# Decoder block on one core: single-use banks for the u and down sums, partition moves by GpSimd DMAs, and a scheduler charge for changes of TensorE's shape

## The chip, the cores and the metric

One core of a Trainium2 chip. The metric is device microseconds of one execution; three runs of the kernel before gave 388.19 to 389.34 us, median 389.16. The profile is of one further execution.

## The reference, cut

One layer on x of 256 tokens by 1024 channels, in float32. A projection gives Q, K, V (512 columns each), u (512) and two gates (1024 each). Q and K get a rotary turn of 16 of each head's 64 dimensions; attention is causal over one block of 256, 8 heads. u goes through a diagonal state-space model (S5, 32 groups of 16 channels, 64 states), a gelu and a gated unit:

```python
proj = h @ w_in[l]
q, k, v, u, g_attn, g_ssm = jnp.split(proj, splits, axis=-1)
attn = moba_attention(q, k, v)
...
y = (jnp.einsum('ghp,bsgp->bsgh', c_re, h_re) - jnp.einsum('ghp,bsgp->bsgh', c_im, h_im) + d_skip * uf)
y = jax.nn.gelu(y.reshape(bsz, seq, SSM_WIDTH))
y = y * jax.nn.sigmoid(y @ w_glu)
...
merged = sigmoid(g_attn) * (attn @ w_attn_proj[l]) + sigmoid(g_ssm) * (ssm @ w_ssm_proj[l])
mix = merged @ w_out[l]
h = layer_norm(DEEPNORM_ALPHA * h + mix, ln1_g[l], ln1_b[l])
up = causal_depthwise_conv(h @ w_up[l], conv_w[l], conv_b[l])
val, gate = jnp.split(up, 2, axis=-1)
ff = (jax.nn.gelu(gate) * val) @ w_down[l]
h = layer_norm(DEEPNORM_ALPHA * h + ff, ln2_g[l], ln2_b[l])
```

## The kernel before, in words

**Products.** Most products are made in three parts: ACT copies a float32 tile to float32r (`hi`), DVE subtracts it from the tile (`lo`), and TensorE (PE) sums hi x hi, lo x hi and hi x lo (`split_to`, L486; `three`). Weights arrive by 512 KB loads from SP into a ring of three raw buffers and are split into a ring of hi/lo pairs (`chunk`). The u projection alone is made in plain float32 (`u_sum`): 8 k tiles by 4 sums of 128 x 256, each product passing the array four times.

**Banks.** PSUM is held as six one-bank tiles and one tile of two banks, `twin`. `J` is the first two banks (bank_61 and bank_62 in orders), `AT` the next three (63 to 65), `S5` the two halves of `twin` and bank_66. The four u sums lie in `J` and the two halves of `twin` (L573).

**u and y change partitions.** The state-space part wants groups of 32 channels at other partitions than the projection leaves them. After u is summed, 32 ACT copies of 32 x 128 bring it from PSUM to `uc` (L711 to L717), splitting even from odd tokens on the way. `e_operand` and `toeplitz` make the SSM's operands out of transposes and small float32 products; `ssm_unit` (L882, four of them) multiplies `uc` side by side on halves of the array into `twin`, and DVE scans. `ssm_out` (L912, two halves) sums y and evicts each half with 16 ACT gelus of 32 x 128, to other partitions and interleaved tokens again. `y` is then split to hi and lo for the gated unit.

**The tail.** The down projection's sums are `dacc` (L1141): two of 512 columns for the first 128 tokens, in AT[0] and AT[1]; 512, 256 and 256 columns for the rest, in AT[2] and the two halves of `twin`. The products of the last few tiles are made part by part, and each part is evicted by DVE (`gm`, scalar_tensor_tensor) into the last layer norm.

**What sets the order.** All operations are recorded first (`Recorder`, L104). A dependence is found by the region of memory (`_region`, L87), in PSUM by the bank of 512 floats; an engine that reads a bank and another that writes it follow each other. `forward` (L156) then plays the engines through with a cost for each operation, and of several such orders the one that ends first is issued, engine by engine. So a changed cost, bank or operation moves instructions all over the program. DVE and GpSimd (Pool) are taken to exclude each other (`SHARED`, L151). In the trace nearly every DVE instruction is of L300, ACT's of L376, matmuls of L395 (sums), L414 (single), L423 (side by side), transposes of L430, SP's loads of L441.

Of the kernel before, what the change touches and what calls it, by code (L numbers as in the profile page):

```python
# [20 lines left out]
P = 128  # L21
# [65 lines left out]
def _region(ap):  # L87
    row = ap.ap[0][0]
    lo = ap.offset % row
    if _in_psum(ap):  # L90

        end = lo + sum((n - 1) * s for s, n in ap.ap[1:])
        return (ap.tensor.name, 0, P, lo // 512 * 512, end // 512 * 512 + 512)
    return (ap.tensor.name, ap.offset // row, ap.offset // row + ap.ap[0][1],
            lo, lo + sum((n - 1) * s for s, n in ap.ap[1:]) + 1)


class Op:
    __slots__ = ("i", "eng", "fn", "cost", "dur", "func", "dma", "group", "preds", "succs", "start", "end")


class Recorder:
# [4 lines left out]
    def add(self, eng, fn, outs, ins, cost, dur=None, func=None, group=None):  # L107

        o = Op()
        o.i, o.eng, o.fn, o.cost, o.func = len(self.ops), eng, fn, cost, func  # L110
        o.dur, o.dma, o.group = dur, dur is not None, group
        o.preds, o.succs = set(), []
        for write, aps in ((False, ins), (True, outs)) if group is None else ((True, outs), (False, ins)):
            for ap in aps:
                t, p0, p1, a, b = _region(ap)
                psum = _in_psum(ap)
                log = self.mem.setdefault(t, [])
                keep = []
                for e in log:
                    q0, q1, c, d, j, w = e  # L120
                    if q0 < p1 and p0 < q1 and c < b and a < d:
                        if w and write and group is not None and self.ops[j].group is group:
                            keep.append(e)
                            continue
                        if (w or write or (psum and self.ops[j].eng != eng)) and j != o.i:
                            o.preds.add(j)
                        if write and p0 <= q0 and q1 <= p1 and a <= c and d <= b:
                            continue
                    keep.append(e)
                keep.append((p0, p1, a, b, o.i, write))  # L130
                self.mem[t] = keep
            if group is not None and write:

                if group.before is None:
                    group.before = set(o.preds)
                o.preds |= group.before
        o.preds.discard(o.i)
        self.ops.append(o)
        return o
# [16 lines left out]
    def forward(self, key, wait=0.0, margin=0.0):  # L156


        ops = self.ops
        left = [len(o.preds) for o in ops]  # L160
        ready_at = [0.0] * len(ops)
        engs = sorted({o.eng for o in ops})
        free = dict.fromkeys(engs, 0.6)
        cand = {e: [] for e in engs}
        table, dma = None, 0.0

        cold, win, busy = True, 0, 0.0
        for o in ops:
            if not left[o.i]:
                cand[o.eng].append(o.i)  # L170
        done = 0
        while done < len(ops):
            best = None
            for e in engs:
                if cand[e]:
                    t = max(free[e], min(ready_at[i] for i in cand[e]))
                    if best is None or t < best[0]:
                        best = (t, e)
            t, e = best
            c = cand[e]  # L180
            if e == "SP":
                i = min(c)
            else:
                i = min((i for i in c if ready_at[i] <= t + 0.02), key=lambda i: (key[i], i))
                if wait:
                    until = t + wait * ops[i].cost
                    j = min((i for i in c if ready_at[i] <= until), key=lambda i: (key[i], i))
                    if key[j] < key[i] - margin:
                        i = j
            c.remove(i)  # L190
            o = ops[i]
            cost = o.cost
            if o.func in self.SETS and table not in self.SETS[o.func]:
                table = self.SETS[o.func][0]
                cost += 1.3
            t = max(t, ready_at[i])
            if e == "PE":
                n = int(t / self.WINDOW)
                if n != win:
                    use = busy / self.WINDOW  # L200
                    cold = n > win + 1 or use < 0.42 or (cold and use < 0.75)
                    win, busy = n, 0.0
                if cold:
                    cost *= 2
                busy += min(t + cost, (win + 1) * self.WINDOW) - t
            o.start = t
            free[e] = t + cost
            if e in self.SHARED:

                e2 = self.SHARED[e]  # L210
                free[e2] = max(free[e2], t + cost)
            if o.dma:
                dma = max(dma, t + cost + 0.65) + o.dur
                o.end = dma + 0.93
            else:
                o.end = t + cost
            done += 1
            for j in o.succs:
                ready_at[j] = max(ready_at[j], o.end + self.latency(o, ops[j]))
                left[j] -= 1  # L220
                if not left[j]:
                    cand[ops[j].eng].append(j)
        return max(o.end for o in ops)
# [158 lines left out]
class Pe:  # L382
# [34 lines left out]
    def side_by_side(self, rounds):  # L417


        def issue():  # L420
            for products in rounds:
                for o, l, r, start, stop in products:
                    self.real.matmul(o, l, r, start=start, stop=stop)  # L423

        flat = [q for products in rounds for q in products]
        self.rec.add("PE", issue, [q[0] for q in flat], [x for q in flat for x in q[1:3]],
                     0.1 + sum(0.12 + 1.17e-3 * max(_free(q[0][0]), 128) for q in rounds))

    def transpose(self, o, a, eye):
        self.rec.add("PE", lambda: self.real.transpose(o, a, eye), [o], [a, eye], 0.109)  # L430


class Dma:
# [13 lines left out]
def block_kernel(ctx: ExitStack, tc: tile.TileContext, w, xtok, small, lnv, out):  # L447
# [1 line left out]
    rec = Recorder()  # L449
    V, G = Vec(rec, nc.vector), Gps(rec, nc.gpsimd)  # L450
    A, T = Act(rec, nc.scalar), Pe(rec, nc.tensor)
    SP = Dma(rec, nc.sync)

    pool = ctx.enter_context(tc.tile_pool(name="pool", bufs=1))
    ps = ctx.enter_context(tc.tile_pool(name="ps", bufs=1, space=PSUM))
# [19 lines left out]
            self.items = [i for i in self.items if not any(i is j for j in items)]  # L475

    J, AT, S5 = banks[0:2], banks[2:5], [twin[:, 0], twin[:, 1], banks[5]]
    pj, at, s5 = Ring(J), Ring(AT[2:] + AT[:2]), Ring(S5)
    pjw = Ring([J[0], S5[2], J[1], AT[0], AT[1]])
    pju = Ring([J[0], J[1], S5[2]])  # L480

# [88 lines left out]
    hilo.more(late[0], late[1])  # L570


    u_acc = J + S5[0:2]  # L573
    xr = gt

    def x_piece(k0, k1):
# [131 lines left out]
    tt(tau_l, tau, tau_h, SU)  # L708


    for q in range(4):  # L711
        for i4 in range(4):
            i = 4 * q + i4
            for j in range(2):
                b0 = 64 * (i % 2) + 32 * j
                src = u_acc[q][32 * i4:32 * i4 + 32, j:S:2]
                A.copy(uc[b0:b0 + 32, i // 2], src)  # L717

# [156 lines left out]
            A.copy(tz[r0, ms, 32:64], pv[r0, :, par, 1])  # L877
            tt(tz[r1, ms, 32:64], pv[r1, :, par, 0], di[r1, ms], AD)

    y = again(et[0], (4, S))  # L880

    def ssm_unit(un):  # L882

# [28 lines left out]
    def ssm_out(big):  # L912
# [4 lines left out]
        def term(n, k, par):  # L917
# [3 lines left out]
            if n == 2:  # L921
# [4 lines left out]

        T.side_by_side([[term(n, k, par) for par in range(2)] for k in range(4) for n in range(2)]
                       + [[term(2, k, par) for par in range(2)] for k in range(4)])
        for k in range(4):
            for par in range(2):  # L930
                i = 8 * big + 2 * k + par
                for j in range(2):
                    b0 = 64 * par + 32 * j
                    c0 = 32 * (i % 4)
                    A.activation(y[c0:c0 + 32, i // 4, j:S:2],
                                 py[par][b0:b0 + 32, k * P:(k + 1) * P], AF.Gelu_apprx_tanh)


    mask = col("mask").unsqueeze(1).to_broadcast([P, 2, P])
# [83 lines left out]
    yh, yl = yhl[:, 0], yhl[:, 1]  # L1023
    sh, sl = shl[:, 0], shl[:, 1]
    for k in range(4):
        split_to(yh[:, k], yl[:, k], y[:, k])
    for cc in range(2):
        hi, lo = chunk(C_GLU + cc)
        for mi in range(2):
            m = 2 * cc + mi  # L1030
            acc = pj()
            def wk(k):
                c = slice(k * 256 + mi * P, k * 256 + (mi + 1) * P)
                return hi[:, c], lo[:, c]
            T.product(acc[:, :S], three(wk, lambda k: (yh[:, k], yl[:, k]), range(4)))
            th_ = tmp["cvv"]()
            A.activation(th_, acc[:, :S], AF.Tanh, scale=0.5)
            stt(th_, th_, 1.0, y[:, m], op0=AD, op1=MU)
            split_to(sh[:, m], sl[:, m], th_)


# [96 lines left out]

    conv = col("conv").rearrange("p (m k) -> p m k", k=4)
    DCOLS = [[(0, 512), (512, 1024)], [(0, 512), (512, 768), (768, 1024)]]  # L1140
    dacc = [[AT[0], AT[1]], [AT[2], S5[0][:, 0:256], S5[1][:, 0:256]]]  # L1141
    d_sum = [[T.sum(b) for b in q] for q in dacc]


# [39 lines left out]
        if LAG <= i < NF - LAST + LAG:  # L1184
            down(i - LAG, all_parts)

    for part in all_parts:
        for i in range(NF - LAST, NF):
            down(i, [part])


    halves = [slice(nh * 512, (nh + 1) * 512) for nh in range(2)]
# [118 lines left out]
```

## Time and profile before

| what | value |
|---|---|
| median of three runs | 389.16 us (388.19 to 389.34) |
| the profiled execution, its own time | 389.81 us |
| its span | 387.4 us |
| PE, DVE, ACT busy, share of the span | 95%, 81%, 62% |
| granted TensorE clock, mean | 0.992 |

A row of a timeline or group gives the engine, the line, the operation with output and inputs by the program's names, the shape, and in brackets the engine's idle time just before it with what ended it. A matmul row's busy time runs from the first start to the last (modelled) end, and records overlap, so paces are taken from start to start. A record with 256 columns of plain float32 stands for half a product.

### The profile page before, as it was taken

Reading aid. Unit: us, or ns where it says so; the run is one execution under the profiler, and the core shown is the slowest. Engines: PE = TensorE matmul, PEld = TensorE weight load, DVE = VectorE, ACT = ScalarE, POOL = GpSimd, SP = SyncE. Lnnn points to the kernel's source line nnn. Section 1 sums busy time; section 2 is a strip of 40 time slices with the busy share of each in tenths; the row PEclk is TensorE's granted clock in tenths of the full one; section 3 lists DMA queues with packets and bytes.
Section 4 is the critical chain, followed back from the end, with each engine's and each line's share of the span. In section 5 each row is a group of like instructions: output and inputs, shape, how many; then the busy total and the mean of one; then the engine's idle time right before and its main releaser. Section 6 shows DMA issues by size and latency. Waiting matters only on the chain.

```text
span 387.4 us, 7089 instructions
## 1 busy us (share of the span) xinstructions
PE 369.7 (95%) x2734; PEld 338.3 (87%) x2734; DVE 314.2 (81%) x580; ACT 240.1 (62%) x447; POOL 7.1 (2%) x48
## 2 busy tenths in 40 slices
PE   7899999999999999999899999999999999999990
PEld 6677777889889999979899999999999999999970
DVE  4979768999699967978999997777776777777775
ACT  3489988957997567622637656555555556555620
POOL 6000000000000000000000000000000000000000
PEclk9999999999999999999999999999999999999996
DMA  7913565413533653698157775545465645554002
GB/s 264 360 61 113 194 216 183 164 57 144 184 111 115 227 203 108 196 338 283 36 170 229 248 239 187 199 164 207 175 197 187 212 168 186 195 180 146 2 0 108
DMA packets 19184, 67.35 MB, mean 174 GB/s; under 512 B 2256, under 2 KB 2512, under 8 KB 19152
## 3 DMA queue, kind: packets, MB, share of 16 engines
q1 hardware_dynamic: 19152, 66.91, 50.1%
q8 instruction: 21, 0.34, 0.3%
q14 instruction: 11, 0.09, 0.1%
HBM read 65.86 MB, written 1.05 MB: 173 GB/s over the span
## 4 chain that ended last, share of the span: by engine, by line
PE 62%; DVE 15%; ACT 13%; DMA 7%; issue 2%; SPq 1%; DVEq 0%; ACTq 0%
PE bank L395 54%; DMA raw<-w 7%; PE twin L395 5%; DVE wl L300 3%; ACT wh L376 3%; ACT et L376 2%; PE bank L423 1%; DVE gm L300 1%; ACT uc L376 1%; SPq L441 1%; ACT L376 1%; ACT p L376 1%; DVE sa L300 1%; ACT gm L376 1%; DVE qk L300 1%
## 5 line engine op out<-in xcount | busy, mean ns | idle before, releaser
L300 DVE TENSOR_TENSOR wl<-raw,wh 128x1024 fp32r<-128x1024 f32 x65 | 79.2, 1223 | 11.3 <-ACT wh L376 11.2
L376 ACT ACTIVATE wh<-raw 128x1024 fp32r<-128x1024 f32 x65 | 68.0, 1053 | 16.7 <-PE bank L395 7.9
L300 DVE SCALAR_TENSOR_TENSOR qk<-bank,sml,qk 128x255 f32<-128x255 f32 (+1 forms) x88 | 42.0, 482 | 26.8 <-ACT qk L376 25.3
L376 ACT ACTIVATE qk<-bank,sml 128x256 f32<-128x256 f32 x44 | 24.8, 565 | 57.7 <-PE bank L395 57.7
L395 PE MATMUL bank<-shl,wh 128*128 128x256 f32 x336 | 48.1, 281 | 0.0
L395 PEld LDWEIGHTS bank<-shl,wh 128*128 128x128 f32 x336 | 42.9, 188 | 0.5
L395 PE MATMUL bank<-yhl,wh 128*128 128x256 f32 x304 | 42.9, 280 | 0.0
L395 PE MATMUL bank<-yhl,wl 128*128 128x256 f32 x288 | 39.8, 279 | 0.0
L395 PEld LDWEIGHTS bank<-yhl,wh 128*128 128x128 f32 x304 | 38.8, 188 | 0.1
L395 PEld LDWEIGHTS bank<-yhl,wl 128*128 128x128 f32 x288 | 36.3, 189 | 0.0
L395 PE MATMUL bank<-wh,xh 128*128 128x512 f32 (+1 forms) x102 | 31.3, 376 | 0.6 <-ACT wh L376 0.5
L395 PE MATMUL bank<-wh,xl 128*128 128x512 f32 (+1 forms) x102 | 29.7, 367 | 0.0
L395 PE MATMUL bank<-wl,xh 128*128 128x512 f32 (+1 forms) x102 | 29.2, 371 | 0.0
L300 DVE TENSOR_TENSOR wl<-ctab,wh 128x1024 fp32r<-128x1024 f32 x18 | 22.0, 1222 | 1.9 <-ACT wh L376 1.8
L395 PEld LDWEIGHTS bank<-wh,xh 128*128 128x128 f32 x102 | 17.7, 188 | 4.4 <-ACT wh L376 1.5
L395 PEld LDWEIGHTS bank<-wh,xl 128*128 128x128 f32 x102 | 18.1, 188 | 2.9
L376 ACT ACTIVATE xh<-stab 128x1024 fp32r<-128x1024 f32 x14 | 14.7, 1051 | 9.1 <-PE twin L395 9.1
L395 PEld LDWEIGHTS bank<-wl,xh 128*128 128x128 f32 x102 | 17.3, 188 | 3.2 <-DVE wl L300 0.4
L376 ACT ACTIVATE wh<-ctab 128x1024 fp32r<-128x1024 f32 x18 | 18.9, 1052 | 1.7 <-PE twin L395 1.5
L300 DVE TENSOR_TENSOR xl<-stab,xh 128x1024 fp32r<-128x1024 f32 x14 | 17.1, 1223 | 1.9 <-ACT xh L376 1.9
L395 PE MATMUL bank<-yhl,xh 128*128 128x256 f32 (+1 forms) x96 | 16.1, 305 | 0.5 <-ACT yhl L376 0.5
L395 PE MATMUL bank<-shl,xh 128*128 128x256 f32 (+1 forms) x96 | 16.5, 300 | 0.0
(288 smaller groups left out, 753.5 us busy)
## 6 DMA issues: line engine op xcount, KB each, us to landing
raw<-w SPq DMA_DIRECT2D x74, 512.0 KB, 3.5
stab<-w SPq DMA_DIRECT2D x20, 512.0 KB, 3.4
ctab<-w SPq DMA_DIRECT2D x19, 512.0 KB, 3.7
gt<-lnv SPq DMA_DIRECT2D x4, 512.0 KB, 5.5
el<-w SPq DMA_DIRECT2D x2, 512.0 KB, 8.3
el<-xtok SPq DMA_DIRECT2D x2, 512.0 KB, 4.0
sml<-small SPq DMA_DIRECT2D x1, 800.0 KB, 10.4
out<-gm SPq DMA_DIRECT2D x3, 256.0 KB, 2.0
```

The costliest lines, as they stand in the source:

```text
L300: self.rec.add(self.eng, lambda: f(o, *args, **kw), [o], ins, self.base + more + n * rate)
L376: self.rec.add("ACT", lambda: f(o, a, func, **kw), outs, ins, cost, func=func.name)
L395: self.pe.real.matmul(self.o, l, r, start=self.done == 0, stop=self.done == self.n - 1)
L423: self.real.matmul(o, l, r, start=start, stop=stop)
L441: self.rec.add("SP", lambda: self.real.dma_start(o, a), [o] if sb_out else [], [a] if sb_in else [], 0.45, dur=P / 16 * max(0.06, 0.027 + ...
```

## The change

**Regions and banks.** A PSUM tile longer than one bank (only `twin`) counts as one region. The u sums move to `J`, bank_66 and bank_64. The ring of `s5` has bank_66 and the first half of `twin`. In the tail, the first 128 tokens' two sums of 512 columns have the two halves of `twin`, made together; the three others have a bank of `AT` each.

**Moves.** u is copied by four ACT copies of 128 x 256 into free room of `gt` (even tokens, then odd), and eight GpSimd DMAs of 32 partitions x 4 x 128 carry it to `uc`. y's half 0 has two gelus of 64 x 512 into `yg` (free room of a qk buffer) and eight GpSimd DMAs of 32 x 2 x 128. Half 1 keeps its 16 gelus, which now write runs of 128. y holds even tokens, then odd, and is read with strided views.

**The planner.** PE pays 0.09 us for each change of (output partitions, input partitions); the side-by-side round's own 0.1 goes. A GpSimd DMA does not block DVE in the plan, and lands 1.9 us after its transfer.

```diff
@@ _region
+        if row > 512:
+            return (ap.tensor.name, 0, P, 0, row)
...
@@ forward
+                if o.kind != kind:
+
+                    kind, cost = o.kind, cost + 0.09
...
-            if e in self.SHARED:
+            if e in self.SHARED and not o.dma:
...
-                o.end = dma + 0.93
+                o.end = dma + (0.93 if e == "SP" else 1.9)
...
+class Gdma:
...
+    def move(self, o, a):
+        n = 1
+        for d in a.shape[:-1]:
+            n *= d
+        self.rec.add("Pool", lambda: self.real.dma_start(o, a), [o], [a], 1.0, dur=n / 16 * 0.06)
...
-    pj, at, s5 = Ring(J), Ring(AT[2:] + AT[:2]), Ring(S5)
+    pj, at, s5 = Ring(J), Ring(AT[2:] + AT[:2]), Ring([S5[2], S5[0]])
...
-    u_acc = J + S5[0:2]
+    u_acc = J + [S5[2], AT[1]]
...
+    uj = gt[:, 8:12].rearrange("p q (j c) -> p q j c", j=2)
     for q in range(4):
-        for i4 in range(4):
-            i = 4 * q + i4
-            for j in range(2):
-                b0 = 64 * (i % 2) + 32 * j
-                src = u_acc[q][32 * i4:32 * i4 + 32, j:S:2]
-                A.copy(uc[b0:b0 + 32, i // 2], src)
+        A.copy(uj[:, q], u_acc[q][:, 0:S].rearrange("p (c j) -> p j c", j=2))
+    for i4 in range(4):
+        for j in range(2):
+            b0 = 64 * (i4 % 2) + 32 * j
+            GD.move(uc[b0:b0 + 32, i4 // 2:8:2], uj[32 * i4:32 * i4 + 32, :, j])
...
+        for par in range(2):
+            r = slice(64 * par, 64 * par + 64)
+            A.activation(yg[r], py[par][r].rearrange("p (k c) -> p k c", k=4), AF.Gelu_apprx_tanh)
+        for k2 in range(2):
+            for par in range(2):
...
+                    b0, c0 = 64 * par + 32 * j, 32 * (2 * k2 + par)
+                    GD.move(y[c0:c0 + 32, 0:2, j], yg[b0:b0 + 32, k2:4:2])
...
-        split_to(yh[:, k], yl[:, k], y[:, k])
+        split_to(by_token(yh[:, k]), by_token(yl[:, k]), natural(y[:, k]))
...
-    dacc = [[AT[0], AT[1]], [AT[2], S5[0][:, 0:256], S5[1][:, 0:256]]]
+    dacc = [S5[0:2], [AT[0], AT[1][:, 0:256], AT[2][:, 0:256]]]
...
-    for part in all_parts:
+    for parts in [all_parts[0:2]] + [[part] for part in all_parts[2:]]:
         for i in range(NF - LAST, NF):
-            down(i, [part])
+            down(i, parts)
```

PE at the end of u, before (`gt` holds x, `el` and `stab` the u weights; bank_63 and bank_64 take Q's two sums):

```order
L395 MATMUL twin<-gt,stab 128x256
L395 MATMUL bank_62<-gt,el 128x256
L395 MATMUL twin<-gt,el 128x256 x4
L395 MATMUL bank_62<-gt,el 128x256 x3
L395 MATMUL bank_63<-yhl,xh 128x512
L395 MATMUL bank_64<-yhl,xh 128x512
L395 MATMUL bank_63<-yhl,xh 128x512
L395 MATMUL bank_64<-yhl,xh 128x512
```

The same place now:

```order
L403 MATMUL bank_66<-gt,el 128x256 x3
L403 MATMUL bank_61<-gt,el 128x256
L403 MATMUL bank_62<-gt,el 128x256
L403 MATMUL bank_64<-gt,el 128x256
L403 MATMUL bank_61<-gt,el 128x256
L403 MATMUL bank_62<-gt,el 128x256
L403 MATMUL bank_64<-gt,el 128x256 x2
L403 MATMUL bank_63<-yhl,xh 128x512 x2
L403 MATMUL bank_63<-yhl,xl 128x512
L403 MATMUL bank_64<-yhl,xh 128x512 x2
```

Each u sum now has a bank that nothing else shares; the last products of bank_61 and bank_62 stand further back, among Q's; Q's second sum takes bank_64 after a u sum.

ACT at that place, before (`wh_71` and `shl` are splits of weights, `stab` and `gk` steps of the SSM's tables):

```order
L376 ACTIVATE yhl<-raw_68 128x1024
L376 ACTIVATE uc<-bank_61 32x128 x2
L376 ACTIVATE uc<-twin 32x128 x7
L376 ACTIVATE shl<-raw_69 128x1024
L376 ACTIVATE uc<-twin 32x128 x9
L376 ACTIVATE wh_71<-raw_70 128x1024
L376 ACT_TABLE_LOAD
L376 ACTIVATE stab<-ga,onepi 128x512
```

And now (`gm<-sml` is an operand of y's sums):

```order
L384 ACTIVATE yhl<-raw_68 128x1024
L384 ACTIVATE gt<-bank_66 128x256
L384 ACTIVATE gm<-sml 64x16x16 x4
L384 ACTIVATE shl<-raw_69 128x1024
L384 ACTIVATE gt<-bank_64 128x256
L384 ACTIVATE wh_71<-raw_70 128x1024
L384 ACTIVATE wh_73<-raw_68 128x1024
L384 ACTIVATE et_85<-sa 64x32x16
```

Two copies of a whole sum stand where 18 small ones stood; those of bank_61 and bank_62 stand some twenty rows further back.

DVE at the tail, before (`gm` is the sum with the residual, `st_158` the statistics of the second 128 tokens):

```order
L300 SCALAR_TENSOR_TENSOR gm<-el,bank_65 128x512
L300 TENSOR_TENSOR nq_153<-rsd_152 128x1
L300 BN_STATS st_158<-gm 128x6
L300 TENSOR_SCALAR sc<-nq_153,ve_151 128x7
L300 SCALAR_TENSOR_TENSOR sd<-sc,sgr 128x8
L300 SCALAR_TENSOR_TENSOR gm<-el,twin 128x256
...
L300 SCALAR_TENSOR_TENSOR gm<-el,twin 128x256
```

And now:

```order
L308 SCALAR_TENSOR_TENSOR gm<-el,bank_63 128x512
L308 TENSOR_SCALAR rsd_152<-ve_151 128x1
L308 BN_STATS st_158<-gm 128x6
L308 TENSOR_TENSOR nq_153<-rsd_152 128x1
L308 SCALAR_TENSOR_TENSOR gm<-el,bank_64 128x256
...
L308 SCALAR_TENSOR_TENSOR gm<-el,bank_65 128x256
```

The last two parts are read from a bank each where both were read from `twin`. GpSimd, which issued memsets alone, now has the eight moves of u in a row and the eight of y among the memsets for the layer norms' tables.

More of the change, by code (lines that the diff above doesn't have):

```diff
@@ L98 @@
 class Op:
-    __slots__ = ("i", "eng", "fn", "cost", "dur", "func", "dma", "group", "preds", "succs", "start", "end")
+    __slots__ = ("kind", "i", "eng", "fn", "cost", "dur", "func", "dma", "group", "preds", "succs", "start", "end")
 class Recorder:
@@ L111, in add @@
         o.dur, o.dma, o.group = dur, dur is not None, group
+        o.kind = (outs[0].shape[0], ins[0].shape[0]) if eng == "PE" else None
         o.preds, o.succs = set(), []
@@ L167, in forward @@
         cold, win, busy = True, 0, 0.0
+        kind = None
         for o in ops:
@@ L426, in side_by_side, with __init__ @@
         self.rec.add("PE", issue, [q[0] for q in flat], [x for q in flat for x in q[1:3]],
-                     0.1 + sum(0.12 + 1.17e-3 * max(_free(q[0][0]), 128) for q in rounds))
+                     sum(0.12 + 1.17e-3 * max(_free(q[0][0]), 128) for q in rounds))
     def transpose(self, o, a, eye):
         self.rec.add("PE", lambda: self.real.transpose(o, a, eye), [o], [a, eye], 0.109)
+class Gdma:
+    def __init__(self, rec, real):
+        self.rec, self.real = rec, real
+    def move(self, o, a):
[3 more added lines that the diff above has]
+        self.rec.add("Pool", lambda: self.real.dma_start(o, a), [o], [a], 1.0, dur=n / 16 * 0.06)
 class Dma:
@@ L451, in block_kernel @@
     A, T = Act(rec, nc.scalar), Pe(rec, nc.tensor)
-    SP = Dma(rec, nc.sync)
+    SP, GD = Dma(rec, nc.sync), Gdma(rec, nc.gpsimd)
     pool = ctx.enter_context(tc.tile_pool(name="pool", bufs=1))
@@ L878, in toeplitz, with natural, by_token @@
             tt(tz[r1, ms, 32:64], pv[r1, :, par, 0], di[r1, ms], AD)
-    y = again(et[0], (4, S))
+    y = again(et[0], (4, 2, NCH))
+    yg = again(qk.items[0], (4, NCH))
+    def natural(ap):
+        return ap.rearrange("p j c -> p c j")
+    def by_token(ap):
+        return ap.rearrange("p (c j) -> p c j", j=2)
     def ssm_unit(un):
@@ L928, in ssm_out @@
                        + [[term(2, k, par) for par in range(2)] for k in range(4)])
-        for k in range(4):
+        if big:
+            for k in range(4):
+                for par in range(2):
+                    for j in range(2):
+                        b0, c0 = 64 * par + 32 * j, 32 * (2 * (k % 2) + par)
+                        A.activation(y[c0:c0 + 32, 2 * big + k // 2, j], py[par][b0:b0 + 32, k * P:(k + 1) * P],
+                                     AF.Gelu_apprx_tanh)
+            return
+        for par in range(2):
+            r = slice(64 * par, 64 * par + 64)
+            A.activation(yg[r], py[par][r].rearrange("p (k c) -> p k c", k=4), AF.Gelu_apprx_tanh)
+        for k2 in range(2):
             for par in range(2):
-                i = 8 * big + 2 * k + par
                 for j in range(2):
[L933 to L936, printed above, removed]
+                    b0, c0 = 64 * par + 32 * j, 32 * (2 * k2 + par)
+                    GD.move(y[c0:c0 + 32, 0:2, j], yg[b0:b0 + 32, k2:4:2])
     mask = col("mask").unsqueeze(1).to_broadcast([P, 2, P])
@@ L1037, in block_kernel @@
             A.activation(th_, acc[:, :S], AF.Tanh, scale=0.5)
-            stt(th_, th_, 1.0, y[:, m], op0=AD, op1=MU)
+            stt(by_token(th_), by_token(th_), 1.0, natural(y[:, m]), op0=AD, op1=MU)
             split_to(sh[:, m], sl[:, m], th_)
```

## Prediction

> **What bounds the kernel now.** I read the page first, then a table of windows cut where the work changes, then the timeline of PE and the groups of ACT. The page's busy line:
>
> ```profile
> PE 369.7 (95%) x2734; PEld 338.3 (87%) x2734; DVE 314.2 (81%) x580; ACT 240.1 (62%) x447; POOL 7.1 (2%) x48
> ```
>
> PE is busy for 95% of the span, so only its idle and badly used time can be won. The windows say where that is (length; busy time and records of PE, PEld, DVE, ACT, POOL; granted clock; DMA share; GB/s):
>
> ```profile
> 9.47:15.59 6.12, 6.12 (x28) 5.33 (x29) 5.40 (x39) 2.43 (x6) 0.00 (x0) 1.00 1.02 421
> 15.59:22.42 6.83, 5.20 (x22) 3.31 (x20) 6.80 (x12) 4.20 (x14) 0.00 (x0) 1.00 0.43 156
> 22.42:69.55 47.13, 44.27 (x234) 35.07 (x233) 37.17 (x65) 44.32 (x90) 0.00 (x0) 1.00 0.49 166
> 69.55:140.00 70.45, 70.36 (x656) 65.20 (x656) 66.88 (x122) 52.64 (x123) 0.37 (x9) 1.00 0.42 145
> 196.00:374.17 178.17, 178.17 (x1330) 169.45 (x1330) 139.12 (x209) 103.31 (x155) 0.00 (x0) 1.00 0.52 178
> ```
>
> From 196 to 374 us (the FFN) PE never idles, at clock 1.00: nothing there can be won. The loss sits in the second and third rows: 15.59 to 22.42 (end of the u projection, PE idle 1.63 us) and 22.42 to 69.55 (Q, K, V and the SSM's operands), where ACT is busy 44.32 of 47.13 us, 94%, and PE 44.27. PE's timeline at the end of u (start, busy, operation, idle before and its releaser):
>
> ```profile
> 17.94 0.70 PE L395 MATMUL twin<-gt,el 128*128 128x256 f32 x2 [0.48 <-ACT uc L376]
> 19.28 0.70 PE L395 MATMUL twin<-gt,el 128*128 128x256 f32 x2 [0.64 <-ACT uc L376]
> 20.34 1.13 PE L395 MATMUL twin<-gt,el 128*128 128x256 f32 x4 [0.36 <-ACT uc L376]
> ...
> 22.42 1.28 PE L395 MATMUL bank<-yhl,xh 128*128 128x512 f32 x4
> ```
>
> Products into the twin tile wait three times for ACT's copies of u into uc: the copies of one sum's half and the last products of the other hold each other up, in turns.
>
> **The u sums (term A).** A u product is 2 records. The first window above has 28 of them, 14 products in 6.12 us: 0.437 us each. From 15.59 to 22.42 stand 20 u records, 10 products: 4.37 us at that pace, 6.83 taken, 2.46 lost. After the change each sum has a bank to itself, the copies of the first two begin while the others are summed, and two of the 24 products move into the Q projection, where they fill rather than wait. One wait is new: Q's second sum needs bank_64, which held a u sum and must first be copied. That is one ACT copy of 128x256 (0.38 us, below) and a little: I keep 0.3 us of the 2.46 and count 2.2 won.
>
> Behind it I read PE at the places where the Q, K, V stretch stops:
>
> ```profile
> 41.90 1.07 PE L395 MATMUL bank<-wl,xh 128*128 128x512 f32 x4
> 43.48 1.20 PE L395 MATMUL bank<-yhl,xh 128*128 128x512 f32 x4 [0.50 <-ACT yhl L376]
> ...
> 50.37 0.83 PE L414 MATMUL twin<-gm,er 128*128 128x128 f32 x6
> 51.04 0.60 PE L430 MATMUL bank<-sml,qk 128*128 128x128 f32 x4
> 51.40 0.72 PE L395 MATMUL bank<-wh,xh 128*128 128x512 f32 x2
> 52.94 0.49 PE L414 MATMUL twin<-gm,er 128*128 128x128 f32 x2 [0.83 <-ACT er L376]
> ...
> 57.77 1.08 PE L395 MATMUL bank<-wh,xh 128*128 128x512 f32 x4
> 58.69 1.08 PE L395 MATMUL bank<-wh,xl 128*128 128x512 f32 x4
> ...
> 66.34 1.16 PE L423 MATMUL twin<-uc,el 64*128 64x128 f32 x16
> 67.49 0.49 PE L423 MATMUL bank<-kT,qT 64*128 64x128 f32 x4
> 68.92 0.70 PE L423 MATMUL bank<-kT,qT 64*128 64x256 f32 x4 [0.93 <-ACT kT L376]
> 69.55 2.17 PE L395 MATMUL bank<-xh,yhl 128*128 128x256 f32 x16
> ```
>
> Four products of 512 columns go from 57.77 to 58.69: 0.23 each. Six Toeplitz records take 0.67 us (0.112 each), four transposes 0.36 (0.09). From 9.47 to 69.55 the code has 24 u products (10.5 us at 0.437), 144 of 512 columns (Q, K, V: 8 k tiles, 2 token tiles, 3 products; 33.1), 32 Toeplitz (3.6), 32 transposes (2.9), the side-by-side round (66.34 to 67.49, 1.15) and the scores (about 1.0): 52.2 us in a stretch of 60.1. So 7.9 us are lost there, 2.46 of them in u. Three of the others are named by a wait: 41.90 to 43.48 took 1.58 for four products worth 0.92 (0.66 lost), 51.40 to 52.94 took 1.54 for two worth 0.46 (1.08), 67.49 to 68.92 took 1.43 for four records worth about 0.45 (0.98). All three end on ACT, which has work queued all the time. What the change takes off ACT:
>
> ```profile
> L376 ACT ACTIVATE gt<-bank 128x256 f32<-128x256 f32 x16 | 6.1, 382 | 5.8 <-PE bank L395 5.3
> ...
> L376 ACT ACTIVATE uc<-twin 32x128 f32<-32x128 f32 x16 | 4.3, 269 | 2.7 <-PE twin L395 2.4
> L376 ACT ACTIVATE uc<-bank 32x128 f32<-32x128 f32 x16 | 4.3, 268 | 0.2
> ```
>
> The 32 copies of u (4.3 + 4.3 = 8.6 us) go, four of 128x256 come (1.5): ACT has 7.1 us less to do ahead of 69.55. So its three waits shrink: I count 0.6 of the 0.66, 0.3 of the 1.08 (the er copies also wait for DVE's tables) and 0.8 of the 0.98, 1.7 in all. The remaining 2.7 us of the loss are changes of shape and small gaps, mostly behind ACT too; half of them, 1.3, I let go. Term A: 2.2 + 1.7 + 1.3 = **-5.2 us**. Its ends: -1.5 (only part of u's own loss is won and DVE, 37.17 us busy in 47.13, takes ACT's place) and -6.7 (only 1.2 of the 7.9 stay). At -5.2, with about 3.0 of it behind 22.42, DVE's 37.17 have to fit in 44.1 us, 84%: room enough, if its inputs come in time.
>
> **The moves.** Eight GpSimd DMAs bring u from its copies to uc, 32 partitions each; Pool is free there (0.00 busy in the third window). They first serve the side-by-side round at 66.34. ACT's last copies of u in this trace:
>
> ```profile
> 36.29 0.55 ACT L376 ACTIVATE uc<-bank 32x128 f32<-32x128 f32 x2
> ```
>
> They end at 36.84. With 28 small copies fewer ahead of them and Q earlier, I put the last at about 33 (an estimate: 36.84 less what is left of the 7.1 us after the work that ACT's new order puts ahead), and the round at 66.34 - 5.2 = 61, so some 28 us remain for the moves. No row has a GpSimd DMA. The nearest are SP's issue of the small load and its landing:
>
> ```profile
> 2.10 0.43 SPq L441 DMA_DIRECT2D sml<-small  x1
> ```
> ```profile
> sml<-small SPq DMA_DIRECT2D x1, 24.0 KB, 3.7
> ```
>
> Issue alone gives 8 x 0.43 = 3.5 us; if each had to land before the next, 8 x 3.7 = 29.6. Overlapped issue is the nearer row (SP issues the next load before the last has landed), and even a move of 3 us fits, so I take 0, ending at 0 below (nothing is won by a move itself) and at +1.6 above (29.6 - 28). The eight moves of y's half 0 have the last two units of attention between its gelus and the split that reads y, and I price them at 0 too.
>
> A rule of the Trainium skill speaks against them: SBUF — State Buffer, section "SBUF: two separate sides", says that a GpSimd DMA's descriptors are written through a port pair which GpSimd shares with DVE, and that such a DMA stalls while DVE runs in a two-port mode; its example goes from 620 to 3100 ns. By that figure, an estimate, eight moves would take 24.8 us and still fit. What the trace shows of the lock:
>
> ```profile
> 3.92 2.66 POOL L353 MEMSET gm<- 128x3072 f32 x1
> ```
> ```profile
> 3.83 0.76 DVE L300 TENSOR_TENSOR xl<-gt,xh 128x256 fp32r<-128x256 f32 x2 [2.91 <-ACT xh L376]
> 5.83 0.78 DVE L300 TENSOR_SCALAR ty<-sml 128x16 f32<-128x16 f32 x1 [1.24 <-DMA sml<-small]
> ...
> 7.45 0.17 DVE L300 TENSOR_SCALAR ty<-ty 128x16 f32<-128x16 f32 x1
> ```
>
> Under Pool's memset a tensor_scalar took 0.78 us, ending with the memset, where its like took 0.17; two tensor_tensors ran beside the same memset at 0.38 each. So a lock exists, for some operations; by that rule, the trace agrees. In the moves' window DVE runs mostly tensor_tensors.
>
> **y and the tables (term D).** Half 0's gelus shrink from 16 of 32x128 to 2 of 64x512, but stand apart, with two table loads more:
>
> ```profile
> L376 ACT ACT_TABLE_LOAD x6 | 7.7, 1283 | 2.3 <-DVE gt L300 1.5 <-PEq L1303 0.7
> ...
> L376 ACT ACTIVATE et<-twin 32x128 f32<-32x128 f32 x24 | 6.7, 278 | 0.3
> ```
>
> 16 x 0.278 = 4.4 us less, 2 x about 0.55 (from 0.382 for 256 columns above) and 2 x 1.28 = 3.7 more: ACT is even. It is 75% busy from 69.55 to 140 (52.64 of 70.45), but DVE is 95% (66.88) and PE 99.9%, so a late softmax there shows. Twelve instructions read y with a stride; no row prices that. I take +0.5, ends 0 and +2.6 (both loads bare).
>
> **The tail (term B).**
>
> ```profile
> 376.06 0.28 PE L395 MATMUL twin<-wh,xl 128*128 128x256 f32 x1
> 376.84 0.39 PE L395 MATMUL twin<-wl,xh 128*128 128x256 f32 x1 [0.51 <-DVE gm L300]
> ```
> ```profile
> 376.37 0.43 DVE gm L300
> 376.84 1.81 PE twin L395 x13
> ```
>
> The last sum's products wait until DVE has read the other half of its tile: 376.06 to 376.84, 0.78, for a step of 0.14 (13 records in 1.81), 0.64 lost. After the change the last two sums have banks of their own, and the twin's halves are both summed before they are read. DVE's read then falls under PE's next sum. I take **-0.6**, ends 0 and -0.78.
>
> **W_out (term C).**
>
> ```profile
> 176.65 0.51 PE L395 MATMUL bank<-wh,xh 128*128 128x256 f32 x2 [0.47 <-ACT wh L376]
> ```
>
> The load of lnv comes a few places later among SP's loads, so this weight may come earlier; I take 0, ends 0 and -1.0. The charge for changes of shape alters the order alone; PE changes shape 28 times in both orders, counted there, so it has no term of its own.
>
> The sum: -5.2 - 0.6 + 0.5 = -5.3. The profiled execution took 389.81, 0.65 above the median of 389.16; 389.81 - 5.3 = 384.5 there, **383.9** against the median.
>
> **Rivals.** *The gain is only local.* DVE becomes the limit from 22 to 69 as ACT is freed; only u (-2.2) and the tail (-0.6) are won: -2.8, 386.4. For it: DVE's 37.17 us and its tables, which er waits for. Against: all waits named there are ACT's.
>
> *No change within 0.3% (about what a measurement of this kernel can tell from none, 1.2 us).* The wait on the twin returns as a wait on bank_64 and the table loads (+2.6) eat the rest: -2.2 - 0.6 + 2.6 = -0.2, 389.0. For it: Q's second sum has the same kind of dependence on ACT. Against: ACT's new order has two copies of 128x256 ahead of that point where 18 of 32x128 stood.
>
> *Slower: the moves come late.* The side-by-side round needs all eight, and behind it PE's in-order queue stops, attention with it. It decides from 28/8 = 3.5 us a move for the first loss; each 1 us a move more costs 8. To undo 5.3 it takes (28 + 5.3)/8 = 4.2 us; at 5 us a move, if landings follow one another and DVE's lock adds to 3.7, it is 40 - 28 = +12, less 5.3: 395.9. For it: the lock in the row of 0.78; against: a DMA's issue row of 0.43, and 28 us.
>
> *More is won*: A at -6.7, B at -0.78, C at -1.0, D at 0: 389.16 - 8.5 = 380.7.
>
> **How the numbers follow.** The forecast has 0.55, local gain 0.19, no change 0.10, slower 0.13, more won 0.03. The forecast's own range, by A between -3.5 and -6.7 and D's and C's ends, is 381 to 387. The range that leaves out no more than 2 in 10 takes local gain and no change in: 381.0 to 389.6. Faster by over 0.3% is 0.55 + 0.19 + 0.03 = 0.77, same 0.10, slower 0.13.
>
> **What would show it.** Right: the last u product starts a run into Q without waits on uc; Q's first product near 20 rather than 22.42; the first gates near 64 to 65 rather than 69.55; from there all starts shifted by the same 4 to 5 us; no wait of 0.51 in the last sums. Wrong: a wait of the side-by-side round on a Pool DMA (the slow rival); ACT idle and DVE at over 90% between 20 and 64 (local gain); a new wait of PE for bank_64's copy over 0.5 us; idle time of PE on softmax between 64 and 135 next to a table load (term D).

## The result, and the profile after

The changed kernel takes 382.50 us in the median of four runs (381.97 to 383.31), the kernel before 389.06 (388.19 to 389.34): a ratio of 0.9837, 95% interval 0.9813 to 0.9861, or 6.6 us less. The profiled execution went from 389.81 to 382.28, its span from 387.4 to 380.5.

The page's busy line and four windows of the changed kernel (length; busy time and records of PE, PEld, DVE, ACT, POOL; granted clock; DMA share; GB/s):

```profile
PE 367.6 (97%) x2734; PEld 339.5 (89%) x2734; DVE 312.0 (82%) x580; ACT 231.8 (61%) x407; POOL 15.9 (4%) x64
```
```profile
15.59:22.42 6.83, 6.83 (x32) 5.71 (x31) 6.69 (x12) 5.58 (x11) 0.00 (x0) 1.00 0.49 182
22.42:65.00 42.58, 42.05 (x231) 33.80 (x230) 37.70 (x76) 40.79 (x80) 4.49 (x8) 1.00 0.55 181
...
190.00:368.00 178.00, 178.00 (x1333) 169.45 (x1332) 136.59 (x204) 102.97 (x155) 0.00 (x0) 1.00 0.52 178
368.00:380.50 12.50, 3.42 (x29) 3.21 (x27) 9.18 (x27) 0.03 (x1) 0.00 (x0) 0.80 0.23 85
```

PE no longer idles between 15.59 and 22.42, and idles 0.53 us between 22.42 and 65 where it idled 2.86 in 47.13. ACT is still 96% busy there; DVE is at 89%. PE's timeline:

```profile
13.14 6.21 PE L403 MATMUL bank<-gt,el 128*128 128x256 f32 x28
19.00 0.80 PE L403 MATMUL bank<-yhl,xh 128*128 128x512 f32 x2
...
31.55 1.03 PE L403 MATMUL bank<-gt,el 128*128 128x256 f32 x4
...
45.73 1.16 PE L422 MATMUL bank<-gm,er 128*128 128x128 f32 x8 [0.41 <-ACT er L384]
...
55.64 0.93 PE L431 MATMUL bank<-kT,qT 64*128 64x128 f32 x8
...
59.92 1.16 PE L431 MATMUL twin<-uc,el 64*128 64x128 f32 x16
...
64.09 1.47 PE L403 MATMUL bank<-xh,yhl 128*128 128x256 f32 x11
```

28 u records (14 products) run from 13.14 to 19.00, 0.42 each, without a stop. Q follows at 19.00 (22.42 before) and doesn't wait for bank_64; the two late u products sit at 31.55. The scores no longer wait for kT, and the side-by-side round at 59.92 doesn't wait for uc, though DMAs now bring it. Gates begin at 64.09, 5.46 us earlier.

For a comparison of all runs I gave each PE record a nominal time (u product 0.427, 512 columns 0.229, 256 columns 0.1135, transposes and Toeplitz 0.109, side by side 0.054 for 128 columns and 0.107 for 256), summed to 346.3 us in each kernel, and cut every trace where the sum passes 10, 15, 60, 160, 170 and 300. So each column holds the same amount of work (not always the same products, since the order differs), in us taken (start; end of u; Q, K, V and SSM operands; gates to most of W_out; layer norm; FFN; tail):

```
kernel                    0-10   10-15  15-60  60-160 160-170 170-300  300-end
before                   16.33    7.43  50.92  108.86   13.27  133.28   57.31
changed                  16.22    5.15  48.11  107.06   14.08  133.00   56.88
small copies of u        17.90    5.03  49.37  110.10   12.40  133.00   56.82
before + banks           17.01    5.04  51.19  107.98   12.38  133.00   56.80
before + moves of u      15.23    5.05  49.75  107.83   13.27  133.81   57.15
u in twin again          16.61    5.11  48.01  107.78   13.18  133.00   57.41
no charge                15.65    5.08  48.23  107.59   14.04  133.00   56.51
old tail sums            15.89    5.15  48.20  107.53   13.06  133.00   56.57
no charge, old tail      15.40    5.10  49.32  108.38   13.06  133.00   56.53
region per bank          15.71    5.15  49.17  107.65   14.06  133.00   57.36
16 small gelus           16.16    5.52  48.38  110.21   13.06  133.00   58.17
y's moves by ACT         16.46    5.15  48.35  108.79   13.07  133.00   57.27
u's moves by SP          17.43    5.12  47.59  108.60   12.56  133.00   57.00
64 moves                 16.00    5.15  61.97  107.26   13.06  133.00   56.76
```

Changed minus before: -0.1, -2.3, -2.8, -1.8, +0.8, -0.3, -0.4, together -6.9, the difference of the spans.

What Pool did (its timeline, and the queues by issue: operation, count, KB, us to landing):

```profile
33.61 4.49 POOL L451 DMA_DIRECT2D uc<-gt  x8 [26.39 <-ACT gt L384]
```
```profile
uc<-gt POOLq DMA_DIRECT2D x8, 64.0 KB, 3.3
et<-qk POOLq DMA_DIRECT2D x8, 32.0 KB, 2.4
```

Eight moves take Pool 4.49 us, 0.56 each; the last was issued near 37.5 and landed near 41, 19 us ahead of the round at 59.92.

The tail (PE, then DVE) and the layer norm's stall, after and then before:

```profile
369.35 0.29 PE L403 MATMUL bank<-xl,athl 128*128 128x256 f32 x1
369.47 0.28 PE L403 MATMUL bank<-wh,xh 128*128 128x256 f32 x1
```
```profile
370.92 0.75 DVE L308 SCALAR_TENSOR_TENSOR gm<-et,rsd,gt 128x512 f32<-128x512 f32 x1
371.59 0.41 DVE L308 SCALAR_TENSOR_TENSOR gm<-el,bank 128x256 f32<-128x256 f32 x1
```
```profile
183.20 2.66 PE L422 MATMUL bank<-sb,gm 128*128 128x128 f32 x16 [1.82 <-DVE sb L308]
```
```profile
189.85 2.05 PE L414 MATMUL bank<-sb,gm 128*128 128x128 f32 x16 [1.43 <-DVE sb L300]
```

PE passes from the second last sum to the last in 0.12 us, where such a step took 0.78. But DVE reads the last sum only at 371.59: it has a 0.75 us step (`gm`, 370.92) in hand, so not all of PE's gain reaches the end. The layer norm stalls PE for 1.82 instead of 1.43.

### The profile page after: what moved, and what is told of

Same layout as the page of the kernel before. It is cut to its first block, busy times and chain, and to the rows that moved or that the text cites. A ratio compares the mean times of both kernels' runs of the same rounds, so it can differ in the third digit from the quotient of the medians.

```text
span 380.5 us, 7089 instructions
## 1 busy us (share of the span) xinstructions
PE 367.6 (97%) x2734; PEld 339.5 (89%) x2734; DVE 312.0 (82%) x580; ACT 231.8 (61%) x407; POOL 15.9 (4%) x64
## 4 chain that ended last, share of the span: by engine, by line
PE 77%; DVE 9%; ACT 7%; DMA 5%; SPq 1%; issue 1%; DVEq 0%
PE bank L403 64%; PE twin L403 8%; DMA raw<-w 4%; PE bank L431 2%; DVE gm L308 2%; ACT wh L384 1%; DMA ctab<-w 1%; SPq L462 1%; ACT L384 1%; DVE wl L308 1%; PE twin L431 1%; DVE sa L308 1%; ACT p L384 1%; PE bank L438 1%; PE bank L422 1%
## 5 line engine op out<-in xcount | busy, mean ns | idle before, releaser
L308 DVE SCALAR_TENSOR_TENSOR qk<-bank,sml,qk 128x255 f32<-128x255 f32 x88 | 42.4, 481 | 27.1 <-ACT qk L384 25.7
L403 PE MATMUL bank<-shl,wh 128*128 128x256 f32 x336 | 46.9, 279 | 0.0
L403 PEld LDWEIGHTS bank<-yhl,wl 128*128 128x128 f32 x288 | 36.3, 188 | 0.0
L403 PE MATMUL bank<-wh,xl 128*128 128x512 f32 (+1 forms) x102 | 27.9, 347 | 0.0
L403 PE MATMUL bank<-wh,xh 128*128 128x512 f32 (+1 forms) x102 | 27.8, 347 | 0.0
L403 PE MATMUL bank<-wl,xh 128*128 128x512 f32 (+1 forms) x102 | 27.6, 348 | 0.0
```

What stands on the lines that cost most here:

```text
L308: self.rec.add(self.eng, lambda: f(o, *args, **kw), [o], ins, self.base + more + n * rate)
L403: self.pe.real.matmul(self.o, l, r, start=self.done == 0, stop=self.done == self.n - 1)
```

## The experiments

All times are medians, each taken beside runs of the kernel before on the same chip (388.92 to 389.29 there). Every edit makes the planner order the program anew, so each carries some scatter: stages that an edit can't touch differ by 1 us and more in the table.

**Small copies of u.** The 32 ACT copies are back, the banks kept.

```diff
-        A.copy(uj[:, q], u_acc[q][:, 0:S].rearrange("p (c j) -> p j c", j=2))
...
-            GD.move(uc[b0:b0 + 32, i4 // 2:8:2], uj[32 * i4:32 * i4 + 32, :, j])
...
+                src = u_acc[q][32 * i4:32 * i4 + 32, j:S:2]
+                A.copy(uc[b0:b0 + 32, i // 2], src)
```

> The changed kernel with u brought to uc by the 32 ACT copies of 32 x 128 again; the single-use banks and all else stay. Theory (ACT, 94% busy from 22 to 70 us before, is what the stops of Q, K and V wait for): ACT gets its 7.1 us back, the 1.7 of the named waits and the 1.3 of the small gaps return: 382.5 + 3.0 = 385.5, first gate near 67 instead of 64.09. Rival (the banks alone make the gain, ACT's copies lie beside PE's work): at most 0.5 slower, 382.5 to 383.0, first gate at 64 to 64.6.

386.64 (ratio to before 0.9928, 0.9898 to 0.9958), 4.1 over the changed kernel. In the profiled execution 1.7 of it is the start (17.90 in the table, of which below), which the edit does not touch. The u stage stays at 5.03; the stage from 15 to 60 is 1.3 longer; the one from 60 to 160 is 3.0 longer, with two waits:

```profile
97.67 1.16 PE L431 MATMUL twin<-uc,el 64*128 64x128 f32 x16 [0.93 <-ACT qk L384]
...
174.39 0.51 PE L403 MATMUL bank<-wh,xh 128*128 128x256 f32 x2 [0.54 <-ACT wh L384]
```

So ACT's relief is worth 1.3 us in the stretch where I expected 3.0, and the banks alone are enough for the u stage. Of the three waits before, those for yhl and kT stay away even with the 32 copies back; only the one for er returns, 0.79 here against 0.41 in the changed kernel. The two later waits come in other kernels too and can't be put down to the copies; with the start they carry the total over both forecasts.

**Before with the banks; before with the moves.** One part of the change each, on the old kernel.

```diff
-    u_acc = J + S5[0:2]
+    u_acc = J + [S5[2], AT[1]]
...
-    pj, at, s5 = Ring(J), Ring(AT[2:] + AT[:2]), Ring(S5)
+    pj, at, s5 = Ring(J), Ring(AT[2:] + AT[:2]), Ring([S5[2], S5[0]])
```

> The kernel before with one part of the change: a bank each for the u sums (and the ring of s5 without the second half of twin). The 32 small ACT copies, the tail, y and the charge stay as before. Theory A (either edit alone wins the u stage): 389.0 - 2.6 = 386.4, the stretch from the first u product to the first Q product 2.6 shorter, and nothing behind it. Theory B (ACT's number of copies is what PE waits for): 388.5 to 389.3, Q's first product later than 21.

```diff
-                A.copy(uc[b0:b0 + 32, i // 2], src)
...
+        A.copy(uj[:, q], u_acc[q][:, 0:S].rearrange("p (c j) -> p j c", j=2))
...
+            GD.move(uc[b0:b0 + 32, i4 // 2:8:2], uj[32 * i4:32 * i4 + 32, :, j])
```

> The kernel before with one part of the change: u by four ACT copies and eight GpSimd DMAs. Banks (two u sums in the halves of twin), the tail, y and the charge stay as before. Theory A (the u stage's 2.6 us need both a shared tile and many small copies, so either edit alone wins them, and the moves also free ACT for 1 to 2 us behind): 389.0 - 4.1 = 384.9, Q's first product at 19 to 20. Theory B (the change's own banks are needed): 387.5 to 389, Q's first product at 21 to 22.5.

Banks alone: 385.11 (ratio 0.9896, 0.9868 to 0.9923). Moves alone: 385.06 (0.9886, 0.9860 to 0.9911). The end of u with the banks alone, then with the moves alone:

```profile
17.38 3.62 PE L395 MATMUL bank<-gt,el 128*128 128x256 f32 x16
20.64 1.28 PE L395 MATMUL bank<-yhl,xh 128*128 128x512 f32 x4
```
```profile
18.18 1.03 PE L395 MATMUL twin<-gt,el 128*128 128x256 f32 x4
18.86 1.28 PE L395 MATMUL bank<-yhl,xh 128*128 128x512 f32 x4
```

Neither has a wait there, and both take 5.05 or less in the stage that took 7.43. Theory A holds for the u stage: either edit alone wins all 2.4 us. Behind it they differ: the moves win 1.2 from 15 to 60, the banks nothing (+0.3). That the banks came out at 385.11 and not at 386.4 is not u's doing: 1.8 of their gain lies from 60 to 170 and 0.5 in the tail, which the edit reaches by the order and by the ring of `s5`, from which y's sums take their banks too. So it isn't a test of u's banks alone there.

**u in twin again.** Two sums share twin, the moves stay.

```diff
-        if row > 512:
-            return (ap.tensor.name, 0, P, 0, row)
...
-    u_acc = J + [S5[2], AT[1]]
+    u_acc = J + S5[0:2]
```

> The changed kernel with two of the u sums in the halves of twin again and a region per bank in the planner; moves, ACT's four copies and the tail stay. Theory (sums that share a tile hold up products and copies in turns): about 2.2 us of the u stage come back, 384.7, with PE waits on ACT's gt copies between 15 and 23 us. Rival (the waits came from the number of small copies): with one copy of 0.38 us for each sum at most two waits of 0.4 remain, 382.5 to 383.3.

382.91 (ratio 0.9837, 0.9807 to 0.9868), u stage 5.11: the rival is right, with one copy for each sum sharing costs nothing there. A wait shows in the tail instead:

```profile
364.61 0.50 PE L401 MATMUL twin<-xh,athl 128*128 128x512 f32 x1 [0.78 <-DVE gm L306]
```

**The region rule and the tail's sums.** First the rule alone is taken back (the first two lines of the diff above), then the tail's sums alone.

> The changed kernel with only the planner's rule taken back that twin is one region; u's single banks, the moves and the tail's new sums stay. Theory (the tail's wait went because the planner now knows that the halves share a tile, and not because of the new banks): PE waits 0.7 to 0.95 for DVE between the last products of the two twin halves, the stretch behind the FFN's bulk is about 0.5 longer, 383.0. Rival (the new banks and the pairing of the first two parts removed the wait): no such wait, 382.5 within 0.4.

```diff
-    dacc = [S5[0:2], [AT[0], AT[1][:, 0:256], AT[2][:, 0:256]]]
+    dacc = [[AT[0], AT[1]], [AT[2], S5[0][:, 0:256], S5[1][:, 0:256]]]
...
-    for parts in [all_parts[0:2]] + [[part] for part in all_parts[2:]]:
+    for parts in [[part] for part in all_parts]:
```

> The changed kernel with the down sums of before (two of 512 in AT, 512 in AT, 256 and 256 in the halves of twin) and each part of the tail by itself. Theory: the wait of 0.64 before the last sum returns, 382.5 + 0.6 = 383.1. Rival: the end of the span is DVE's, which took 0.33 longer after PE's last product in the changed kernel than before, so only 0.3 or less returns, 382.5 to 382.8.

Rule away: 383.57 (ratio 0.9839, 0.9811 to 0.9866). Old sums: 381.94 (0.9811, 0.9778 to 0.9843). PE in the first, DVE in the second:

```profile
365.62 0.50 PE L401 MATMUL twin<-xh,athl 128*128 128x512 f32 x1 [0.78 <-DVE gm L306]
```
```profile
369.02 1.42 DVE L308 SCALAR_TENSOR_TENSOR gm<-et,rsd,gt 128x512 f32<-128x512 f32 x2
370.53 0.75 DVE L308 SCALAR_TENSOR_TENSOR gm<-el,twin 128x256 f32<-128x256 f32 x2
```

Without the rule a wait is there with the new sums, now between the two halves of `twin` that the first 128 tokens use; with the rule it is gone with the old ones, since the planner puts both of DVE's reads of twin behind PE's last product. The tails take 57.36 and 56.57, against 56.88 in the changed kernel and 57.31 before. So what the tail won it owes to the rule, and the new sums earn nothing. Half a microsecond is at the edge of what this column can tell, though: the kernel before with the banks has the wait (0.51) and a tail of 56.80. For the old sums both expectations were wrong.

**No charge for changes of shape,** alone and with the old tail sums; the old 0.1 for a side-by-side round comes back with it.

```diff
-                    kind, cost = o.kind, cost + 0.09
+                    kind = o.kind
```

> The changed kernel without the planner's 0.09 us for each change of shape, and with the old 0.1 of a side-by-side round. Theory: the charge changes the order alone and is worth nothing that shows: 382.5, within 0.6. Rival: the better order of the middle (1.5 us won between the first gate and the layer norm, the W_out wait gone) is the charge's: 384.0.

> The changed kernel without the charge for changes of shape and with the tail's sums of before; the rule that twin is one region stays. Theory (neither is worth anything): 381.3 to 382.5, the same as the changed kernel within the scatter, and no PE wait over 0.5 in the last sums. Rival (their effects add, 0.6 and 0.6): 381.3 or less, measurably faster than the changed kernel.

381.84 (ratio 0.9813, 0.9783 to 0.9842) and 382.53 (0.9835, 0.9807 to 0.9864). The charge is worth nothing that shows, and the two don't add.

**Half 0 of y.** By 16 gelus again; then by two gelus, with ACT copies instead of the DMAs.

```diff
-        if big:
+        if True:
```

> The changed kernel with the half 0 of y by 16 gelus of 32 x 128 again (into the new layout), without its eight DMAs. Theory (ACT even: 16 x 0.28 against 2 x 0.55 and two table loads): 382.5, within 0.6. Rival (two loads in the softmax of the busy middle cost what they last): 382.5 - 1.3 = 381.2 or, if the DMAs' freeing of ACT is what pays, 383.8.

```diff
-                    GD.move(y[c0:c0 + 32, 0:2, j], yg[b0:b0 + 32, k2:4:2])
+                    A.copy(y[c0:c0 + 32, 0:2, j], yg[b0:b0 + 32, k2:4:2])
```

> The changed kernel with y's half 0 still evicted by two gelus of 64 x 512, and its eight moves made by ACT copies in SBUF instead of GpSimd DMAs. It tells what the run with 16 small gelus lost 3.7 us by. Theory (the twin bank came free late: one gelu of about 0.55 frees it where eight took 2.24, and the next state-space unit waited 1.52 us for it): the banks come free as early as in the changed kernel, so 382.5 to 383.3, and no wait of over 0.5 before a unit. Rival (ACT's added time is what the middle cannot bear): 385.5 to 386.5.

386.17 (ratio 0.9928, 0.9900 to 0.9955) and 383.59 (0.9874, 0.9841 to 0.9907). PE and ACT with 16 gelus, then PE at the same unit, and ACT, with two:

```profile
97.66 1.16 PE L431 MATMUL twin<-uc,el 64*128 64x128 f32 x16 [1.52 <-ACT et L384]
```
```profile
95.37 2.24 ACT L384 ACTIVATE et<-twin 32x128 f32<-32x128 f32 x8
```
```profile
93.98 1.16 PE L431 MATMUL twin<-uc,el 64*128 64x128 f32 x16 [0.17 <-ACT qk L384]
```
```profile
93.33 0.59 ACT L384 ACTIVATE qk<-twin 64x512 f32<-64x512 f32 x1
```

Eight gelus hold twin for 2.24 us, one of 64 x 512 for 0.59, and the next state-space unit writes twin. With the early release the loss falls from 3.7 to 1.1 though ACT makes the moves; 383.59 is just above the 383.3 that the theory allowed and well below the rival's 385.5. From 60 to 160 the table has 3.1 more with the 16 gelus and 1.7 more with ACT's copies. In the 3.1 lie the unit's wait of 1.52, one of 0.32 behind it, and W_out's wait for its weights:

```profile
171.04 0.51 PE L403 MATMUL bank<-wh,xh 128*128 128x256 f32 x2 [0.17 <-ACT wh L384]
172.32 0.51 PE L403 MATMUL bank<-wh,xh 128*128 128x256 f32 x2 [0.77 <-ACT wh L384]
```

In the 1.7 lie 0.17 for the unit and 0.34 and 0.77 for the same weights. That wait comes and goes with the order (below); without it the late release costs about 2 us and ACT's copies little, so ACT's time isn't the main thing that the middle can't bear. The tail, 1.3 longer with 16 gelus, is not theirs either: PE and DVE end as in the changed kernel, and behind DVE's last row it takes 4.3 us to the end of the span (384.5), where the changed kernel takes 2.9.

```profile
379.23 0.88 DVE L308 SCALAR_TENSOR_TENSOR gm<-gm,rsd,gt 128x256 f32<-128x256 f32 x2
```

**64 moves:** the eight moves of u cut into eight each. Their price in the plan is set to 0.06 each, so that the round stays at its place in PE's order.

```diff
-            GD.move(uc[b0:b0 + 32, i4 // 2:8:2], uj[32 * i4:32 * i4 + 32, :, j])
+            for s in range(0, 32, 4):
+                GD.move(uc[b0 + s:b0 + s + 4, i4 // 2:8:2], uj[32 * i4 + s:32 * i4 + s + 4, :, j], 0.06)
```

> The changed kernel with each of the eight moves of u cut into eight of 4 partitions, 64 in all with the same bytes; the first side-by-side round stays at its place in PE's order. Theory (a move costs Pool 0.56 us whatever its size, and the round at 59.9 us needs the last): 64 x 0.56 = 36 from 33.6, landing 2 later: PE stops until about 71.5, 382.5 + 11.6 = 394. Rival (the price goes by the packets, 512 of them in either case): no change, 382.5.

395.51 (ratio 1.0168, 1.0132 to 1.0204): 13.0 over the changed kernel, 11.6 expected. Pool, then PE:

```profile
33.68 14.25 POOL L451 DMA_DIRECT2D uc<-gt  x25 [26.45 <-ACT gt L384]
48.16 4.02 POOL L451 DMA_DIRECT2D uc<-gt  x7 [0.23 <-issue]
52.34 18.04 POOL L451 DMA_DIRECT2D uc<-gt  x32 [0.16 <-issue]
```
```profile
64.23 0.76 PE L431 MATMUL twin<-uc,el 64*128 64x128 f32 x2 [4.05 <-DMA uc<-gt]
71.85 1.62 PE L431 MATMUL twin<-uc,el 64*128 64x128 f32 x10 [6.86 <-DMA uc<-gt]
```

36.3 us for 64 is 0.57 each: Pool's price goes by the DMA, not by its bytes. (A move makes 32 packets at either size, so a price by packets is not ruled out.) PE stops 10.9 us for them, and behind the stop the granted clock is 0.50 from 71.85 to 75 and 0.84 to 78, so that the gates begin at 77.64, 13.6 later: the stop's price is the wait and about 2.6 us behind it. This is the slow rival of the prediction; eight moves are 4.5 us of the 26 that lie between 33.6 and 59.9.

**u's moves by SP.**

```diff
-            GD.move(uc[b0:b0 + 32, i4 // 2:8:2], uj[32 * i4:32 * i4 + 32, :, j])
+            SPM.move(uc[b0:b0 + 32, i4 // 2:8:2], uj[32 * i4:32 * i4 + 32, :, j])
...
```

> The changed kernel with u's eight moves issued by SP among the loads of weights instead of GpSimd. Theory (what counts is that ACT doesn't make them): 382.5 to 383.5. Rival (GpSimd's own queue is needed, since SP's loads behind the moves wait for u's last copy): PE waits for weights behind the moves, 385 or more.

383.44 (ratio 0.9857, 0.9826 to 0.9887). SP's row:

```profile
33.81 5.24 SPq L451 DMA_DIRECT2D uc<-gt  x8
```

They take SP 0.66 each, and from 15 to 60 the kernel is as fast as any (47.59). In that stretch it counts that ACT is rid of them, not which queue has them.

## Why the prediction was right, and where it wasn't

Forecast -5.3 (383.9); measured -6.6 in the medians and -7.5 between the profiled executions, 6.9 of it in the spans. The likeliest case came, a little larger. The closeness is in part luck: about 1.5 of the 2.8 from 15 to 60 did not come by the reason given, and the middle's 1.8 was not forecast.

- **The u stage (-2.2).** -2.3, and Q begins at 19.00. Size and place are right. The step that named the cause failed: "After the change each sum has a bank to itself" is one of two edits that each suffice. The turns needed a shared tile and many small copies together. The wait for bank_64, 0.3 in the sum, did not come.
- **Q, K and V (-3.0).** -2.8 from 15 to 60. The waits for yhl and kT are gone, that for er fell from 0.83 to 0.41, much as counted. But the moves make only 1.2 to 1.3 of it (both ways of trying it agree), not 3.0. The step that failed is "So its three waits shrink": with the 32 copies back, yhl's and kT's waits stay away, so they went with the new order and not with ACT's relief. They had cost 0.66 and 0.98, about the other 1.5; which part of the change made that order was not traced. ACT's share didn't fall (94 to 96%): in the freed time it now makes the first softmax's exponentials and a second table load before the gates begin, 3.7 us.
- **DVE as the next limit.** It went to 89% and did not take ACT's place.
- **y and the tables (+0.5).** The sign was wrong: the stage from 60 to 160 became 1.8 shorter, and 3.1 longer again with 16 gelus. "ACT is even" counted ACT's time alone; what the two big gelus bring is a shorter hold of twin. W_out's weight wait (term C, taken at 0, end -1.0; 0.47 before) lies in this stage and is gone; other kernels have it or not with no relation to their edits. Nor is y alone in this stage: the kernel before with the moves of u, or with the banks, is 0.9 to 1.0 shorter here with the old gelus. How the 1.8 divides is not settled.
- **The layer norm.** Not in the sum: +0.8. DVE delivers later (1.82 against 1.43) and the clock dips behind it, as below, about 1.0. Against these, twelve records that took 2.35 us before, from 194.00 to 196.35 (0.12 each is the pace elsewhere), have no like in the changed kernel. What is left of the 0.8 is not traced.
- **The tail (-0.6).** -0.4: the wait went, and DVE's own work at the end kept a part. The cause was wrong: "the last two sums have banks of their own" is worth nothing without the planner's rule.
- **The moves (0).** Right, with 19 us to spare. DVE's lock, the other half of the slow rival, was not put to the test by the eight: while they ran, from 33.6 to 38.1, DVE ran tensor_tensors and scalar_tensor_tensors and nothing else, and they took 0.56 each; the last of the 64, issued while DVE stood idle, took 0.56 too. With 0.57 us a move and 2.8 for the landing (the 64 moves' median) the slow rival begins at about (26.3 - 2.8) / 0.57 = 41 moves.

## What to carry to other kernels

When an evictor and the products of the next sum take turns on one tile, look for both conditions, a shared tile and many small reads, and remove the cheaper one; removing both pays once. Price an eviction by how long it holds its bank as well as by its engine's time. Under a planner an edit also buys a new order, worth 1 us either way here, so compare equal stretches of work and not totals alone.

## What the runs showed that was not expected

**The start's pace differs from trace to trace.** The first u products, with the small copies and then in the kernel before with the moves:

```profile
5.02 5.35 PE L403 MATMUL bank<-gt,ctab 128*128 128x256 f32 x12 [0.86 <-DMA ctab<-w]
10.21 2.75 PE L403 MATMUL bank<-gt,stab 128*128 128x256 f32 x12
```
```profile
4.50 1.10 PE L395 MATMUL bank<-gt,ctab 128*128 128x256 f32 x4 [0.34 <-DMA ctab<-w]
5.44 1.03 PE L395 MATMUL twin<-gt,ctab 128*128 128x256 f32 x4
```

Six products took 5.2 us in the one, 0.86 each; two took 0.94 in the other, 0.47 each. In the first the weight came 0.5 us later, but that isn't a rule: the changed kernel's first product came at 4.31 and its first eight took 5.00 us, while with a region per bank it came at 4.71 and they took 3.69. The granted clock reads 1.00 in all of them; the cause is open. The stage from 0 to 10 varies from 15.23 to 17.90, a range as wide as that of several runs of one kernel (382.68 to 386.25 for y's moves by ACT); that it is the cause of that scatter is not shown.

**The clock after a stall.** Behind the layer norm, before and after:

```profile
191.60:194.70 3.10, 3.10 (x25) 2.93 (x24) 3.10 (x9) 0.91 (x3) 0.00 (x0) 1.00 0.48 174
```
```profile
185.50:188.60 3.10, 3.10 (x19) 3.10 (x19) 3.10 (x9) 0.84 (x2) 0.00 (x0) 0.62 0.50 174
```

Behind an idle time of 1.82 us the granted clock was 0.62 in the mean of these 3.1 us (0.50 from 185 to 187), 19 records where 25 fit; behind 1.43 it was 1.00. Other kernels with the same 1.82 show the dip (no charge, region per bank: 14.04 and 14.06 from 160 to 170) or don't (old tail sums, 64 moves: 13.06), and behind the 2.05 of u in twin again there is none: the same wait costs 1.0 us more or not, and what decides it is open.
